# Wider products, a stacked gate operand and one mask for four heads, in a two-layer float32 decoder trunk

## The chip, the cores and the metric

One core of a Trainium2 chip runs the whole program in one launch. The metric is device time in microseconds, the median of several runs. Float32 matrices are multiplied as split pairs: `hi` is the operand rounded to float32r, which TensorE multiplies in a single pass, `lo` is what rounding left, and three products (hi x hi, hi x lo, lo x hi) are added up in PSUM. [...]

## The reference, cut to what matters

The input is 1024 tokens by 1024 features. Layer A is attention with three branches, a pooling mixer and an MLP; layer C is gated linear attention and an MLP. Two places matter here.

```python
# layer A, compressed branch: 63 compressed keys, 8 heads, groups of 4 heads share keys
s_c = einsum('bghqd,bgcd->bghqc', qb, kc)
p_c = masked_softmax(s_c, cmp_end[None, :] <= t[:, None])
o_c = einsum('bghqc,bgcd->bghqd', p_c, vc)

# layer C, projections and decay
h = x @ w_in
q_, k_, v_, r, a = split(h, (512, 512, 1024, 1024, 16))
loga = log_sigmoid(a @ gate_w2 + gate_b) / 16
b = cumsum(loga within a chunk of 64)
q_t, k_t = q * exp(b), k * exp(-b)
...
out = (o * rsqrt(mean(o**2) + eps) * norm_g * silu(r)) @ w_out
```

## The kernel before, in words

The program is written as Python loops on named tiles; a scheduler then sets each engine's order from a model of its own and adds the waits. So a loop's body is not one stretch of the trace: a later step's matmuls may stand between an earlier step's. A tile that has several buffers (`bufs=`) is written again when the last reader of that buffer is done.

**Attention (`attention`, `scores`).** The loops run over 8 query blocks of 128 tokens, two key groups and three branches. In the compressed branch (L483 to L503) the four heads of a group fill a PSUM tile `s` of 4 x 64 columns. `Q2` holds a head's scaled queries split, `hi` on 64 rows and `lo` on the other 64; `K2C` holds the compressed keys twice over the rows, as a rounded part and a rest. So a head takes one product with each part (L489, L490), which multiplies hi and lo of the query at once, and a third (L491), identity times a slice of the constant `cb`, which adds -1e30 to masked keys. `compress` (L387) makes `K2C` with one copy and one subtraction.

**Layer C, its start.** The preceding MLP ends with the first two feature-major weights of layer C. Then `layer_c` opens the pool `wC` and loads what it needs: the decay weights `GW` (16 rows `gate_w2`, one row `gate_b`, L1018 and L1019), the norm gains `ng` (L1021), and then weight after weight. `weight` (L81) loads a piece into a buffer of the tag `rawt`, ACT rounds it into `hit`, DVE subtracts into `lot`. There are 3 buffers of `rawt` and 4 each of `hit` and `lot`. Loads are issued by SP, in order.

**Layer C, projections.** Six feature-major weights (L1059) come first. The token-major ones (L1074) are 8: the first has 272 columns (256 of V and the 16 gate inputs `a`, kept in `A16`), the others 256. Each is cut into two or three pieces of up to 4 x 256 columns. For every weight the loop runs over 8 token blocks; `token_major` issues 24 products (8 blocks of the contraction times three), with the activations stationary and the weight streaming:

```python
for k in range(KB):
    wh, wl = w[k]
    self.mm3(ps, self.xh[half][:, k, ts], self.xl[half][:, k, ts], wh, wl, k == 0, k == KB - 1)
```

Weights 0 to 3 are copied to `VV` by ACT (L1084). Weights 4 to 7 make the output gate: tanh on ACT (L1087), two operations on DVE (L1088, L1089), a store to `gr_d` (L1090).

**Layer C, decay.** With the third weight `decay` (L1023) is called for each token block: TensorE transposes `A16` (L1029), DVE sets `AT` to 1 and copies the transpose into its 16 upper rows, TensorE multiplies `AT` (17 rows) by `GW` in plain float32 (L1034), ACT and DVE take the log-sigmoid, four float32 products with a triangle of ones (L1047) give the cumulative sums, ACT the exponentials, POOL scales queries and keys.

Of the kernel before, what the change touches and what calls it, by code (L numbers as in the profile page):

```python
# [16 lines left out]
P = 128  # L17
S = 1024
D = 1024
# [10 lines left out]
C_ID, C_CAUS, C_WIN, C_CMP, C_T, C_VAL, C_MH, C_INV, C_KEEP, C_N = 0, 128, 256, 384, 512, 643, 644, 645, 709, 837  # L30
# [23 lines left out]
class Body:  # L54
    def __init__(self, tc, io, out):
        self.wbufs = {"rawt": dict(bufs=3), "hit": dict(bufs=4), "lot": dict(bufs=4)}
        self.tc, self.nc, self.io, self.out = tc, tc.nc, io, out
# [153 lines left out]
    def layer_a(self):  # L211
        nc, tc, io, cst, cb = self.nc, self.tc, self.io, self.cst, self.cb
        with ExitStack() as ea:
            self.xa = self.pool(ea, "xa")
            Q2 = [self.xa.tile([P, 8, 512], FR, name=f"Q2_{h}") for h in range(2)]
            K2C = self.xa.tile([P, 2, 2, 64], FR, name="K2C")
            VAC = self.xa.tile([64, 2, P], FR, name="VAC")
            with ExitStack() as ex:
# [4 lines left out]
                psA = self.pool(ex, "psA", bufs=5, space=PSUM)  # L223
# [163 lines left out]
    def compress(self, K2C, VAC, tmp, psA, KC):  # L387
# [10 lines left out]
        nc.vector.memset(K2C[:].bitcast(F32), 0.0)  # L398
        nc.vector.memset(VAC[:].bitcast(F32), 0.0)
        for t in range(2):  # L400
# [26 lines left out]
            if t == 0:  # L427
                nc.tensor.matmul(ps2[:, 0:126], w2[:, 0].rearrange("p a b -> p (a b)"), x[:], start=True, stop=True)
                v = ps2[:, 0:126].rearrange("p (g c) -> p g c", g=2)
                nc.scalar.activation(K2C[:, :, 0, 0:63], v, AF.Copy)  # L430
                nc.vector.tensor_tensor(K2C[:, :, 1, 0:63], v, K2C[:, :, 0, 0:63].bitcast(F32), OP.subtract)
            else:
                for g in range(2):
                    nc.tensor.matmul(ps2[0:63, g * 64:g * 64 + 64], x[:, g * 63:(g + 1) * 63], w2[:, 1, 0], start=True, stop=True)
                v = ps2[0:63, 0:128].rearrange("p (g c) -> p g c", g=2)
                nc.scalar.activation(VAC[0:63, :, 0:64], v, AF.Copy)
                nc.vector.tensor_tensor(VAC[0:63, :, 64:128], v, VAC[0:63, :, 0:64].bitcast(F32), OP.subtract)

    def attention(self, ea, kvp, Q2, K2, VA, gates, CK):
# [4 lines left out]
        with ExitStack() as ex:  # L444
# [28 lines left out]
            def scores(i, g, br):  # L473
# [521 lines left out]
    def layer_c(self, head):  # L995
# [10 lines left out]
        with ExitStack() as ew:  # L1006
# [8 lines left out]
            self.reserve(wp, ("rawt", [P, D], F32, 3), ("hit", [P, D], FR, 4), ("lot", [P, D], FR, 4))  # L1015
# [4 lines left out]
            ng = wp.tile([P, 256], F32, name="ng", bufs=1)  # L1020
            nc.sync.dma_start(ng[:], io["norm_g"].to_broadcast([P, 256]))  # L1021

            def decay(tb):  # L1023
# [50 lines left out]
            for i in range(8):  # L1074
                n, nw = (272, 320) if i == 0 else (256, 256)
                src = io["wC_tm0"] if i == 0 else io["wC_tm"][i - 1]
                w = [(wh[:, 0:n], wl[:, 0:n]) for wh, wl in self.weight(src, [3, 3, 2] if i == 0 else [4, 4], nw, "t")]
                for tb in range(TB):
                    ps = psA.tile([P, 272], F32, name="fm")
# [3 lines left out]
                    if i < 4:  # L1083
                        nc.scalar.activation(VV[tb // 4][:, tb % 4, i * 256:(i + 1) * 256], ps[:, 0:256], AF.Copy)  # L1084
                    else:
                        t = wp.tile([P, 256], F32, name="t", bufs=2)
                        nc.scalar.activation(t[:], ps[:, 0:256], AF.Tanh, scale=0.5)  # L1087
                        nc.vector.scalar_tensor_tensor(t[:], t[:], 1.0, ps[:, 0:256], op0=OP.add, op1=OP.mult)  # L1088
                        nc.vector.scalar_tensor_tensor(t[:], t[:], 0.5, ng[:], op0=OP.mult, op1=OP.mult)  # L1089
                        nc.sync.dma_start(self.gr_d[tb][:, (i - 4) * 256:(i - 3) * 256], t[:])  # L1090
                    if i == 2:
                        decay(tb)
# [150 lines left out]
def lay_out(inputs):  # L1243
# [8 lines left out]
    def km(m):  # L1252
        return m.reshape(KB, P, m.shape[1]).transpose(1, 0, 2)

    io = {}
# [17 lines left out]
    io["wC_tm"] = c(np.stack([km(vr[:, 256 * i:256 * i + 256]) for i in range(1, 8)]))  # L1273
# [33 lines left out]
```

## Time and profile before

| | before |
|---|---|
| three runs | 2336.37, 2332.02, 2336.13 us |
| their median | 2336.13 us |
| profiled execution | 2338.69 us, span 2336.9 us |
| busy: PE, DVE, ACT, POOL | 2248.0, 1469.4, 895.6, 1299.2 us |
| TensorE's mean granted clock | 0.986 of full speed |

Times within the span are counted from its first instruction. A matmul's record is longer than the distance to the next one's start, since matmuls are pipelined. The bracket at a row's end gives the idle time before an instruction and what ended it.

### The profile page before, as it was taken

The page shows a single profiled execution, that of the slowest core. Times are in us where ns is not written, and L with a number is a line of the kernel's source. Part 1 is how long each engine was busy: PE and PEld are TensorE (multiplying, and loading weights), DVE is VectorE, ACT ScalarE, POOL GpSimd, SP SyncE. Part 2 cuts the span into 40 slices and gives each one's busy share as a digit, 9 for nine tenths or more (in the row PEclk, how much of TensorE's full clock was granted, in tenths as well). Part 3 has the DMA queues.
Part 4 walks back from the last instruction along what each step waited for, and adds up shares of the span by engine and source line. Part 5 has one row for each costly group of instructions (what it writes and reads, how often), then busy time and mean ns, then how long its engine had stood idle before and what let it go on. Part 6 is the DMA issues. An engine that isn't in the chain of part 4 may idle for free.

```text
span 2336.9 us, 30957 instructions
## 1 busy us (share of the span) xinstructions
PE 2248.0 (96%) x11346; PEld 1866.6 (80%) x11346; DVE 1469.4 (63%) x2058; ACT 895.6 (38%) x1729; POOL 1299.2 (56%) x955
## 2 busy tenths in 40 slices
PE   8999999998999999999999999989899999999998
PEld 6888777776778877788887999978777888778887
DVE  5622777787766657887671113466676555788776
ACT  4213766664333333444322255222242333344431
POOL 2112766563867765989750012043385776588884
PEclk9999999999999999999999999999999999999999
DMA  5144110004454455644232211222445445474421
GB/s 185 46 145 139 48 41 13 10 10 165 163 162 150 152 200 184 222 142 146 65 129 63 78 37 57 65 105 73 176 153 167 149 149 201 158 258 140 145 73 72
DMA packets 121417, 282.42 MB, mean 121 GB/s; under 512 B 13985, under 2 KB 19361, under 8 KB 121266
## 3 DMA queue, kind: packets, MB, share of 16 engines
q1 hardware_dynamic: 113202, 259.48, 33.6%
q10 hardware_dynamic: 8064, 20.98, 2.4%
q8 instruction: 89, 1.46, 0.3%
q14 instruction: 62, 0.51, 0.1%
HBM read 197.57 MB, written 80.74 MB: 119 GB/s over the span
## 4 chain that ended last, share of the span: by engine, by line
PE 42%; POOL 4%; issue 3%; DVE 2%; DMA 2%; ACT 1%; ACTq 0%; POOLq 0%; SPq 0%; DVEq 0%
PE u L105 6%; PE u L103 6%; PE u L104 6%; PE fm L105 4%; PE fm L103 4%; PE fm L104 4%; PE v L105 3%; PE v L103 3%; PE v L104 3%; POOL op L76 2%; POOL T L902 1%; DVE op L76 1%; PE y L103 1%; PE y L104 1%; PE y L105 1%
## 5 line engine op out<-in xcount | busy, mean ns | idle before, releaser
L76 POOL TENSOR_TENSOR op<-a,op 128x512 fp32r<-128x512 f32 x168 | 272.0, 1642 | 61.3 <-ACT op L75 54.4
L75 ACT ACTIVATE op<-a 128x512 fp32r<-128x512 f32 x168 | 104.3, 621 | 189.6 <-issue 135.5
L105 PE MATMUL u<-op 128*128 128x512 f32 x448 | 173.1, 392 | 3.3 <-POOL op L76 3.2
L104 PE MATMUL u<-op 128*128 128x512 f32 x448 | 171.9, 390 | 1.4 <-DVE op L76 1.4
L103 PE MATMUL u<-op 128*128 128x512 f32 x448 | 170.1, 390 | 0.7 <-DVE XT L918 0.7
L105 PE MATMUL u<-Bt,op 128*128 128x512 f32 x384 | 151.0, 394 | 5.1 <-DVE op L76 5.1
L75 ACT ACTIVATE op<-S 128x512 fp32r<-128x512 f32 x144 | 90.5, 629 | 169.6 <-PE u L105 97.5
L103 PE MATMUL u<-Bt,op 128*128 128x512 f32 x384 | 151.3, 394 | 4.0 <-ACT ev L713 4.0
L104 PE MATMUL u<-Bt,op 128*128 128x512 f32 x384 | 150.7, 392 | 0.0
L105 PE MATMUL fm<-hit,xl 128*128 128x256 f32 (+1 forms) x512 | 145.9, 285 | 0.0
L103 PE MATMUL fm<-hit,xh 128*128 128x256 f32 (+1 forms) x512 | 145.8, 285 | 0.0
L104 PE MATMUL fm<-lot,xh 128*128 128x256 f32 (+1 forms) x512 | 145.0, 283 | 0.0
L76 DVE TENSOR_TENSOR op<-T,op 128x512 fp32r<-128x512 f32 x96 | 117.8, 1233 | 23.8 <-ACT op L75 23.8
L104 PE MATMUL v<-op 128*128 128x512 f32 x336 | 130.1, 390 | 2.4 <-DVE op L76 2.4
L105 PE MATMUL v<-op 128*128 128x512 f32 x336 | 129.9, 390 | 0.6 <-POOL op L76 0.6
L1053 POOL TENSOR_TENSOR QK<-QK,E 128x512 f32<-128x512 f32 x8 | 10.4, 1305 | 209.8 <-ACT E L1049 200.9
L103 PE MATMUL v<-op 128*128 128x512 f32 x336 | 125.7, 390 | 1.0 <-ACT op L75 1.0
L76 POOL TENSOR_TENSOR low<-raww,hiw 128x1024 fp32r<-128x1024 f32 (+1 forms) x22 | 40.6, 1860 | 143.5 <-ACT hiw L75 143.5
L705 POOL TENSOR_TENSOR S<-raw 128x512 f32<-128x512 f32 x64 | 95.7, 1502 | 44.4 <-DVE op L76 42.7
L918 DVE TENSOR_TENSOR XT<-XT,u 128x512 f32<-128x512 f32 x144 | 95.3, 678 | 29.8 <-PE u L105 29.4
L75 ACT ACTIVATE op<-raw 128x512 fp32r<-128x512 f32 x116 | 71.4, 627 | 108.9 <-PE v L105 80.8
L727 DVE SCALAR_TENSOR_TENSOR ev<-ev 128x512 f32<-128x512 f32 x96 | 111.1, 1158 | 2.1
(377 smaller groups left out, 6997.2 us busy)
## 6 DMA issues: line engine op xcount, KB each, us to landing
raw<-in_w_dram SPq DMA_DIRECT2D x72, 512.0 KB, 3.8
S_d<-ev SPq DMA_DIRECT2D x112, 256.0 KB, 2.3
w2r<-in_w_dram SPq DMA_DIRECT2D x56, 512.0 KB, 4.5
A_d<-ev SPq DMA_DIRECT2D x100, 256.0 KB, 2.5
a<-S_d SPq DMA_DIRECT2D x96, 256.0 KB, 2.7
a<-A_d SPq DMA_DIRECT2D x88, 256.0 KB, 2.8
x_d<-xt ACTq DMA_DIRECT2D x16, 512.0 KB, 2.6
raw<-x_d SPq DMA_DIRECT2D x16, 512.0 KB, 4.5
```

The source lines that it names most:

```text
L75: nc.scalar.activation(hi, src, AF.Copy)
L76: (lo_eng or nc.vector).tensor_tensor(lo, src, hi.bitcast(F32), OP.subtract)
L103: mm(out, lh, rh, start=start, stop=False, **kw)
L104: mm(out, lh, rl, start=False, stop=False, **kw)
L105: mm(out, ll, rh, start=False, stop=stop, **kw)
L705: POOL.tensor_tensor(st[p][name], st[p][x], st[p][y], op)
L727: DVE.scalar_tensor_tensor(other[:], other[:], 0.0, other[:], op0=OP.max, op1=OP.mult)
L902: sb[0].tensor_tensor(*sb[1:])
L918: DVE.tensor_tensor(x, x, ps[:], add)
L1053: nc.gpsimd.tensor_tensor(q1, q1, E1[:], OP.mult)
```

## The change

1. **Compressed scores.** `K2C` becomes one float32 tile. For a group one mask product of 256 columns opens the accumulation (the mask's slice is repeated for four heads by its access pattern), and a head takes one product in plain float32 (the query tile is read as float32). `compress` loses the subtraction.
2. **Gate product.** `GW` becomes 96 rows of float32r: rounded weights at row 0 and at row 32, the rest at row 64; unused rows are zero. They are built once, by way of a buffer of the tag `rawt` that is set to zero, filled by six loads, rounded by ACT and subtracted by DVE. `AT` becomes two standing tiles of 96 rows: rounded inputs at 0 and 64, the rest at 32, with ones beside the rounded parts for the bias. One float32r product of 96 rows takes the place of the float32 one of 17.
3. **Token-major weights.** Weights 2 to 7 (256 columns) become three of 512, loaded in four pieces of 2 x 512 columns. What follows them (copy, tanh, the two operations with `ng`, the store) is 512 columns wide; `ng` is loaded twice, side by side. `rawt` has 2 buffers now, `hit` and `lot` 5.

```diff
-        self.wbufs = {"rawt": dict(bufs=3), "hit": dict(bufs=4), "lot": dict(bufs=4)}
+        self.wbufs = {"rawt": dict(bufs=2), "hit": dict(bufs=5), "lot": dict(bufs=5)}
...
+                    mask = cb[:, None, C_CMP + 64 - 8 * i:C_CMP + 128 - 8 * i].to_broadcast([P, 4, 64])
+                    nc.tensor.matmul(s[:, 0:256].rearrange("p (h c) -> p h c", h=4), idb, mask, start=True, stop=False)
                     for hp in range(4):
-                        o = s[:, hp * 64:(hp + 1) * 64]
                         q = Q2[half][:, g * 4 + hp, qs]
-                        nc.tensor.matmul(o, q, K2C[:, g, 0], start=True, stop=False)
-                        nc.tensor.matmul(o, q, K2C[:, g, 1], start=False, stop=False)
-                        nc.tensor.matmul(o, idb, cb[:, C_CMP + 64 - 8 * i:C_CMP + 128 - 8 * i], start=False, stop=True)
+                        nc.tensor.matmul(s[:, hp * 64:(hp + 1) * 64], q.bitcast(F32), K2C[:, g], start=False, stop=hp == 3)
...
-            GW = wp.tile([17, 512], F32, name="GW", bufs=1)
-            nc.sync.dma_start(GW[0:16], io["gate_w2"])
-            nc.sync.dma_start(GW[16:17], io["gate_b"])
...
+            GW = wp.tile([96, 512], FR, name="GW", bufs=1)
+            gw = wp.tile([P, D], F32, name="gw", tag="rawt", bufs=2)
+            nc.vector.memset(gw[0:96, 0:512], 0.0)
+            for r in (0, 32, 64):
+                nc.sync.dma_start(gw[r:r + 16, 0:512], io["gate_w2"])
+                nc.sync.dma_start(gw[r + 16:r + 17, 0:512], io["gate_b"])
+            nc.scalar.activation(GW[:], gw[0:96, 0:512], AF.Copy)
+            nc.vector.tensor_tensor(GW[64:96], gw[64:96, 0:512], GW[64:96].bitcast(F32), OP.subtract)
...
-                AT = wp.tile([17, P], F32, name="AT", bufs=1)
-                nc.vector.memset(AT[:], 1.0)
-                nc.vector.tensor_copy(AT[0:16], ps[0:16, 0:P])
+                AT = ATs[tb % 2]
+                nc.scalar.activation(AT[0:16], ps[0:16, 0:P], AF.Copy)
+                nc.scalar.activation(AT[64:80], ps[0:16, 0:P], AF.Copy)
+                nc.vector.tensor_tensor(AT[32:48], ps[0:16, 0:P], AT[0:16].bitcast(F32), OP.subtract)
...
-            for i in range(8):
...
+            for i, (c, n, nw, ks) in enumerate(((0, 272, 320, [3, 3, 2]), (256, 256, 256, [4, 4])) + tuple((512 * j, 512, 512, [2] * 4) for j in (1, 2, 3))):
+                src = io["wC_tm0"] if i == 0 else io["wC_tm1"] if i == 1 else io["wC_tm"][i - 2]
+                w = [(wh[:, 0:n], wl[:, 0:n]) for wh, wl in self.weight(src, ks, nw, "t")]
```

The scheduler's order at three places, of the program before and of the changed one.

On SP, where layer C starts (`rawt` the raw weights, `wo` the output weights of later), before:

```order
L1070 DMA wo<-in_w_out_c_dram 128x2x1024 x3
L1018 DMA GW<-in_gate_w_dram 16x512
L1019 DMA GW<-in_gate_b_dram 1x512
L1021 DMA ng<-in_norm_g_dram 128x256
L87 DMA rawt<-in_wC_fm_dram 128x512 x12
L87 DMA rawt<-in_wC_tm_dram 128x960 x2
```

and changed:

```order
L1081 DMA wo<-in_w_out_c_dram 128x2x1024 x3
L1031 DMA ng<-in_norm_g_dram 128x256 x2
L1020 DMA gw<-in_gate_w_dram 16x512
L1021 DMA gw<-in_gate_b_dram 1x512
L1020 DMA gw<-in_gate_w_dram 16x512
L1021 DMA gw<-in_gate_b_dram 1x512
L1020 DMA gw<-in_gate_w_dram 16x512
L1021 DMA gw<-in_gate_b_dram 1x512
L87 DMA rawt<-in_wC_fm_dram 128x512 x12
L87 DMA rawt<-in_wC_tm_dram 128x960 x2
```

Six small loads by way of `gw` now stand between the early loads and the first weight; `ng` moved ahead of them.

On PE, where a later weight's first token block ends, with buffer numbers (`fm` the PSUM tile of a token block, `hit` and `lot` the weight's split pieces), before:

```order
L105 MATMUL fm_12590<-hit_12585,xl0_10694 128x256
L103 MATMUL fm_12590<-hit_12585,xh0_10693 128x256
L104 MATMUL fm_12590<-lot_12586,xh0_10693 128x256
L105 MATMUL fm_12590<-hit_12585,xl0_10694 128x256
L103 MATMUL fm_12616<-hit_12579,xh0_10693 128x256
L104 MATMUL fm_12616<-lot_12580,xh0_10693 128x256
L105 MATMUL fm_12616<-hit_12579,xl0_10694 128x256
```

and changed, in the second weight of 512 columns, whose pieces are `hit_12495`, `12501`, `12507` and `12513`:

```order
L104 MATMUL fm_12548<-lot_12496,xh0_10580 128x512
L105 MATMUL fm_12548<-hit_12495,xl0_10581 128x512
L103 MATMUL fm_12548<-hit_12495,xh0_10580 128x512
L104 MATMUL fm_12548<-lot_12496,xh0_10580 128x512
L105 MATMUL fm_12548<-hit_12495,xl0_10581 128x512
L103 MATMUL fm_12548<-hit_12501,xh0_10580 128x512
L104 MATMUL fm_12548<-lot_12502,xh0_10580 128x512
L1045 MATMUL d_12255<-GW_11172,AT1_11184 128x512
L105 MATMUL fm_12548<-hit_12501,xl0_10581 128x512
L103 MATMUL fm_12548<-hit_12501,xh0_10580 128x512
L103 MATMUL fm_12518<-hit_12513,xh0_10580 128x512
```

Before, a block's 24 products follow each other. Now 18 products of the first block have gone, then 10 of the next block and a gate product, before the first one with the fourth piece, `hit_12513`.

On PE, in the compressed scores of a group (`s` the PSUM tile, `cb` the masks), before:

```order
L489 MATMUL s<-K2C,Q_0_244 128x64
L490 MATMUL s<-K2C,Q_0_244 128x64
L491 LDWEIGHTS cb
L491 MATMUL s<-cb 128x64
L489 MATMUL s<-K2C,Q_0_244 128x64
L490 MATMUL s<-K2C,Q_0_244 128x64
L491 LDWEIGHTS cb
L491 MATMUL s<-cb 128x64
```

and changed:

```order
L524 MATMUL s<-cb 128x128
L486 LDWEIGHTS cb
L486 MATMUL s<-cb 128x256
L489 MATMUL s<-K2C,Q_0_244 128x64 x4
L521 MATMUL s<-K2s,Q_0_244 128x256
L522 MATMUL s<-K2s,Q_0_244 128x256
```

Three instructions for each head became one, and four masks one of 256 columns ahead of them.

## Rows read from the trace of the kernel before

**Rows 1.** The page, part 1: busy us, share of the span, instructions.

```profile
PE 2248.0 (96%) x11346; PEld 1866.6 (80%) x11346; DVE 1469.4 (63%) x2058; ACT 895.6 (38%) x1729; POOL 1299.2 (56%) x955
```

**Rows 2.** Windows by time: length, busy us of each engine, PE clock, DMA, GB/s.

```profile
225.00:540.00 315.00, 299.01 (x1820) 235.84 (x1818) 242.34 (x471) 204.54 (x465) 199.07 (x219) 0.98 0.09 33
...
1308.10:1511.40 203.30, 203.30 (x1626) 195.96 (x1624) 55.84 (x107) 82.64 (x166) 20.90 (x16) 1.00 0.16 52
```

**Rows 3.** Timeline of PE: start, us, engine, line, operation; 38 rows between.

```profile
1299.24 0.39 PE L105 MATMUL fm<-xh,lot 128*128 128x512 f32 x1
...
1308.08 0.39 PE L105 MATMUL fm<-xh,lot 128*128 128x512 f32 x1
```

**Rows 4.** Timeline of ACT: one L1087 for each block of 24 narrow products.

```profile
1456.96 0.38 ACT L1087 ACTIVATE t<-fm 128x256 f32<-128x256 f32 x1 [2.13 <-PE fm L105]
...
1464.16 1.06 ACT L75 ACTIVATE hit<-rawt 128x1024 fp32r<-128x1024 f32 x1 [1.06 <-PE fm L105]
...
1511.68 0.38 ACT L1087 ACTIVATE t<-fm 128x256 f32<-128x256 f32 x1 [2.49 <-PE fm L105]
```

**Rows 5.** Timeline of PE around one gate product, L1034.

```profile
1361.01 0.28 PE L104 MATMUL fm<-lot,xh 128*128 128x256 f32 x1
1361.22 1.12 PE L1034 MATMUL d<-GW,AT 17*128 17x512 f32 x2
1362.27 0.39 PE L105 MATMUL fm<-hit,xl 128*128 128x256 f32 x1
1362.49 0.28 PE L103 MATMUL fm<-hit,xh 128*128 128x256 f32 x1
```

**Rows 6.** Timeline of PE, two products of 64 rows.

```profile
521.25 0.51 PE L554 MATMUL o<-th,VAC 64*128 64x512 f32 x1
521.60 0.40 PE L555 MATMUL o<-tl,VAC 64*128 64x512 f32 x1
```

**Rows 7.** Timeline of PE, one head's compressed scores and the next's first.

```profile
231.45 0.28 PE L489 MATMUL s<-K2C,Q 128*128 128x64 f32 x1
...
231.68 0.21 PE L491 MATMUL s<-cb 128*128 128x64 bf16 x1
231.72 0.28 PE L489 MATMUL s<-K2C,Q 128*128 128x64 f32 x1
```

**Rows 8.** Timeline of PE, four float32 products (eight records), the next start.

```profile
1443.64 1.06 PE L1047 MATMUL d<-cst,t__12557 128*128 128x131 f32 x8
1444.45 0.36 PE L103 MATMUL fm<-hit,xh 128*128 128x256 f32 x1
```

**Rows 9.** Timeline of the SP queue before layer C: issues of loads.

```profile
1212.98 0.69 SPq L1018 DMA_DIRECT2D GW<-in_gate_w_dram  x1
1213.72 0.30 SPq L1019 DMA_DIRECT2D GW<-in_gate_b_dram  x1
...
1236.40 8.93 SPq L87 DMA_DIRECT2D rawt<-in_wC_fm_dram  x7
```

**Rows 10.** Timeline of PE, first products of layer C; 13 rows between.

```profile
1240.17 0.80 PE L103 MATMUL fm<-xh,hit 128*128 128x512 f32 x1 [3.71 <-ACT hit L75]
...
1246.15 0.39 PE L103 MATMUL fm<-xh,hit 128*128 128x512 f32 x1
```

**Rows 11.** Chain of waits after the last token-major block: start, us, what.

```profile
1511.68 0.39 ACT t L1087
1512.09 0.43 DVE t L1088
...
1513.17 0.50 DVE att L1110
```

**Rows 12.** Groups on DVE, 1308 to 1512 us: busy us, mean ns | idle.

```profile
L76 DVE TENSOR_TENSOR lot<-rawt,hit 128x1024 fp32r<-128x1024 f32 x14 | 17.9, 1286 | 32.1 <-ACT hit L75 32.1
...
L1039 DVE SCALAR_TENSOR_TENSOR t__12179<-d,t__12179 128x512 f32<-128x512 f32 x1 | 0.7, 692 | 3.2 <-ACT t__12179 L1038 3.2
```

**Rows 13.** DMA issues, 1308 to 1512 us: xcount, KB, us to landing.

```profile
rawt<-in_wC_tm_dram SPq DMA_DIRECT2D x11, 512.0 KB, 4.3
```

More of the change, by code (lines that the diff above doesn't have):

```diff
@@ L215, in layer_a @@
             Q2 = [self.xa.tile([P, 8, 512], FR, name=f"Q2_{h}") for h in range(2)]
-            K2C = self.xa.tile([P, 2, 2, 64], FR, name="K2C")
+            K2C = self.xa.tile([P, 2, 64], F32, name="K2C")
             VAC = self.xa.tile([64, 2, P], FR, name="VAC")
@@ L397, in compress @@
             nc.sync.dma_start(w2[:, :, d], io["cmp_w2"])
-        nc.vector.memset(K2C[:].bitcast(F32), 0.0)
+        nc.vector.memset(K2C[:], 0.0)
         nc.vector.memset(VAC[:].bitcast(F32), 0.0)
@@ L1014, in layer_c @@
             psD = self.pool(ew, "psD", bufs=3, space=PSUM)
-            self.reserve(wp, ("rawt", [P, D], F32, 3), ("hit", [P, D], FR, 4), ("lot", [P, D], FR, 4))
+            self.reserve(wp, ("rawt", [P, D], F32, 2), ("hit", [P, D], FR, 5), ("lot", [P, D], FR, 5))
             A16 = wp.tile([P, TB, 16], F32, name="A16", bufs=1)
-            GW = wp.tile([17, 512], F32, name="GW", bufs=1)
-            nc.sync.dma_start(GW[0:16], io["gate_w2"])
-            nc.sync.dma_start(GW[16:17], io["gate_b"])
-            ng = wp.tile([P, 256], F32, name="ng", bufs=1)
-            nc.sync.dma_start(ng[:], io["norm_g"].to_broadcast([P, 256]))
+            GW = wp.tile([96, 512], FR, name="GW", bufs=1)
[6 more added lines that the diff above has]
+            nc.vector.tensor_tensor(GW[64:96], gw[64:96, 0:512], GW[64:96].bitcast(F32), OP.subtract)
+            ATs = [wp.tile([96, P], FR, name=f"AT{j}", bufs=1) for j in range(2)]
+            for t in ATs:
+                for r, one in ((0, 1.0), (32, 0.0), (64, 1.0)):
+                    nc.vector.memset(t[r:r + 32].bitcast(F32), one)
+            ng = wp.tile([P, 512], F32, name="ng", bufs=1)
+            for j in range(2):
+                nc.sync.dma_start(ng[:, j * 256:(j + 1) * 256], io["norm_g"].to_broadcast([P, 256]))
             def decay(tb):
@@ L1073, in layer_c @@
                 preload_wo()
-            for i in range(8):
-                n, nw = (272, 320) if i == 0 else (256, 256)
-                src = io["wC_tm0"] if i == 0 else io["wC_tm"][i - 1]
-                w = [(wh[:, 0:n], wl[:, 0:n]) for wh, wl in self.weight(src, [3, 3, 2] if i == 0 else [4, 4], nw, "t")]
+            for i, (c, n, nw, ks) in enumerate(((0, 272, 320, [3, 3, 2]), (256, 256, 256, [4, 4])) + tuple((512 * j, 512, 512, [2] * 4) for j in (1, 2, 3))):
+                src = io["wC_tm0"] if i == 0 else io["wC_tm1"] if i == 1 else io["wC_tm"][i - 2]
+                w = [(wh[:, 0:n], wl[:, 0:n]) for wh, wl in self.weight(src, ks, nw, "t")]
                 for tb in range(TB):
-                    ps = psA.tile([P, 272], F32, name="fm")
+                    ps = psA.tile([P, 512], F32, name="fm")
                     self.token_major(w, ps[:, 0:n], tb)
@@ L1082, in layer_c @@
                         nc.vector.tensor_copy(A16[:, tb], ps[:, 256:272])
[L1083 to L1088 removed]
+                        n_ = 256
+                    else:
+                        n_ = n
+                    if i < 3:
+                        nc.scalar.activation(VV[tb // 4][:, tb % 4, c:c + n_], ps[:, 0:n_], AF.Copy)
+                    else:
+                        t = wp.tile([P, 512], F32, name="t", bufs=2)
+                        nc.scalar.activation(t[:], ps[:], AF.Tanh, scale=0.5)
+                        nc.vector.scalar_tensor_tensor(t[:], t[:], 1.0, ps[:], op0=OP.add, op1=OP.mult)
                         nc.vector.scalar_tensor_tensor(t[:], t[:], 0.5, ng[:], op0=OP.mult, op1=OP.mult)
[L1090 removed]
+                        nc.sync.dma_start(self.gr_d[tb][:, c - D:c - D + 512], t[:])
                     if i == 2:
@@ L1272, in lay_out @@
     io["wC_tm0"] = c(km(np.concatenate([vr[:, 0:256], al, np.zeros((D, 48), np.float32)], axis=1)))
-    io["wC_tm"] = c(np.stack([km(vr[:, 256 * i:256 * i + 256]) for i in range(1, 8)]))
+    io["wC_tm1"] = c(km(vr[:, 256:512]))
+    io["wC_tm"] = c(np.stack([km(vr[:, 512 * i:512 * i + 512]) for i in range(1, 4)]))
     io["gate_w2"] = c(a["c_gate_w2"][0])
```

3 lines of the change are left out of this document (1 added, 2 removed).

## The prediction

> **What bounds the kernel now.** I read the page's busy times first: TensorE is busy for 96% of the span [rows 1], so a change pays where it shortens the matmul stream, or costs where that stream must wait. Next I cut the span into stages by time [rows 2]: attention, which holds the compressed scores, has TensorE busy for 299 of 315 us; the token-major projections of layer C have it busy for all of 203.3 us, at a granted clock of 1.00, which is the upper of its two levels, 2.4 GHz. In the second stage nothing else is late, so there each nanosecond off a matmul is a nanosecond off the run. Last came the matmul timeline, read by the distance between starts: durations overlap (0.28 us is shown for products that start every 0.12 us), so a sum of durations would overstate everything. The sum is made against the profiled execution, 2338.69 us (span 2336.9 us and 1.8 us around it). It stands 2.6 us above the median of the three runs, 2336.13 us. A measurement of this kernel tells 0.2%, about 4.7 us, from no change.
>
> **The 512-column weights.** Six weights of 256 columns become three of 512: 6 x 8 token blocks x 24 = 1152 products become 576. One block of 24 narrow products lasts 2.88 us (nineteen of them between the two outer rows, 1456.96 and 1511.68 us) [rows 4], so 0.120 us each. At 512 columns with the same split tiles the distance is (1308.08 - 1299.24) / 39 = 0.2267 us [rows 3]. These are feature-major products: the weight is stationary there and the activation streams, in token-major it is the other way round, but both are 128 rows by 128 columns of the same type. Two narrow ones cost 0.2400 us, one wide one 0.2267: 0.0133 us saved, times 576 is **-7.7 us**. Both widths thus carry about 13.3 ns besides their columns at 2.4 GHz (256 columns are 106.7 ns, 512 are 213.3).
>
> The Trainium skill (TensorE: Matmul & The Clock Gate, section "Back-to-back issue gap") gives that fixed part as about 2.5 ns; by it halving the count would save 576 x 2.5 ns = 1.4 us. The trace disagrees with it at both widths, and I go by the trace.
>
> The copies and gate products on ACT, DVE and the queue become half as many and twice as wide. They lie beside the matmuls (ACT is busy for 83 of the 203 us, DVE for 56 [rows 2]), so I cost them at nothing, except the last one, below.
>
> **The gate product.** A plain float32 product of 17 rows and 512 columns stands in the matmul stream eight times. From the product before it (1361.01) to the second after it (1362.49) pass 1.48 us [rows 5]; without it two steps of 0.12 us would: it costs 1.24 us. Now it is one single-pass product of 96 rows. No row shows 96 rows. Bounds: a full-height product, 0.227 us [rows 3]; and above, a product of 64 rows, which takes 0.35 us until the next start [rows 6], plus 0.09 us on each side for changing height (0.21 instead of 0.12 us before it, 0.22 after it [rows 5]): 0.53 us. I take 0.43 us, one such change, because the 64-row product is the nearest row and its 0.35 us already hold one. Saved 0.81 us, times 8: **-6.5 us** (bounds -5.7 and -8.1). The two copies and the subtraction that build the stacked operand stand on ACT and DVE between the transpose and this product; the changed order leaves products of other tiles between them, and a decay now recurs every 60 to 70 wide products, some 15 us, where it recurred after some 70 narrow ones. I cost them at nothing; if that cover failed, each would add about 0.5 us on TensorE.
>
> The Trainium skill (the same page, section "LDWEIGHTS (loading the stationary operand)") has the weight load depend on columns alone, not on rows. By it 96 rows cost what 128 do, 0.227 us, and the term would be -8.1 us; the 64-row product's 0.35 us speaks against that here.
>
> **The compressed scores.** Before, a head took two products of 64 columns and a mask: 231.45 to 231.72, 0.27 us, so 1.08 us for four heads [rows 7]. Each product takes 0.115 us, far above 64 columns' time, so its weight load must set it. A plain float32 product has two records. Four of them with 131 columns last 0.81 us until the next start [rows 8], 0.10 us per record; with 64 columns no more, and no less than the two single loads they replace unless those get cheaper. So four heads cost 0.81 to 0.92 us, the change of type behind them 0.09 (as on each side of the gate product [rows 5]), and one mask of 256 columns 0.107 to 0.16: 1.01 to 1.17 against 1.08 us. **0 us**, bounds -1.1 and +1.4 over 16 groups. The scheduler also moves neighbours around these products. With 16 us of gaps in this stage that could go either way; I leave 3 us to each side.
>
> **The start of layer C.** The gate weights used to have a small tile of their own, loaded at 1213 us. Now they pass through a buffer of the weight tag `rawt`, and in the built program the memset of that buffer waits for a matmul that stands twelve products before the end of the preceding MLP. Behind it on SP stand six small loads, and behind these the first weight load of layer C, which in the old order was issued at 1236.40 us [rows 9], with TensorE idle until its weight came. Twelve products at 0.12 us are 1.44 us and the old load also waited for the same stream's end, so the memset starts near 1235.1; a DVE memset of 512 columns takes 0.50 us [rows 11]; SP starts near 1235.7. A pair of small loads took 0.69 + 0.30 us with the gap between them, 1.05 us [rows 9]; the long one may have been slowed by 3 MB in flight, so the pair lies between 0.7 and 1.1 us. Three pairs, 2.1 to 3.3 us; the first weight is issued at 1237.8 to 1239.0, I take 1238.6: **+2.2 us** (bounds +1.4 and +2.6). It lands after the rounding of the gate weights on ACT, so that adds nothing. The clock already falls in today's wait of 3.71 us and comes back at 1246.15 [rows 10]; I expect the same after the longer one.
>
> **The end of the projections.** The chain of waits goes on from the last block through ACT and DVE: tanh, two products, memset [rows 11]. They become twice as wide: ACT 0.39 to 0.60 us (+0.2), DVE 0.43 to 0.69 us twice (+0.5; 0.69 is a 128x512 operation of the same kind [rows 12]). What is late next is the same DVE queue. **+0.7 us**, bounds +0.4 and +1.0.
>
> **Sum:** -7.7 - 6.5 + 0 + 2.2 + 0.7 = -11.3 us: 2327.4 against the profiled execution, 2324.8 against the median. I predict **2325 us**.
>
> **The rivals.**
> *The refill holds up the stream (slower).* Each wide weight has four tiles, and there are five buffers for the split tiles and two for raw ones, so the fourth tile is loaded only after the second has been split, and that only after the last token block has freed a buffer. From the start of that block: 6 products (1.36 us), ACT 1.06 [rows 4], DVE 1.29 [rows 12], the load 4.3 [rows 13], ACT 1.06, DVE 1.29: 10.4 us. It is needed after 24 + 18 products of the two blocks and 11 that the new order pulls in between, 12.0 us, plus about 1.0 for a decay: 13.0. The margin is 2.6 us; it is used up when ACT, a strict queue, has a decay with both of its table loads ahead of the split. For: those stand there in the changed order, right ahead of the fourth tile's split. Against: ACT is busy for 41% of the stage, and those exponentials are due before the tile has landed. Each of three refills would then lose some 2.5 us, and the clock's return after a wait about 2.8 us more (14 products at 0.43 instead of 0.23 us [rows 10]): 16 us, 2341 us. Chance 0.06.
> *The width saves only a fixed 2.5 ns per product* [against: rows 3, 4]: 6.3 us less gain, 2331 us. Chance 0.05. It is the case of the skill's rule above.
> *The gate product stays dear:* 96 rows taken in two passes, or its operand late. Half of the gain goes: 2328 to 2331 us. Chance 0.08.
> *Attention is reshuffled for the worse or the better* by more than 3 us, since the moved masks shift what runs beside them: 2330 or 2320 us. Chance 0.05 each.
> *It does not do what it says:* the built program has the fewer, wider products, so I give this no chance of its own.
>
> **How the numbers follow.** My forecast has 0.71. Its own bounds: the gains reach from -15.8 to -13.4 us, attention from -4 to +4, start and handover from +1.8 to +3.6, which makes 2318 to 2331 with all ends added up. The range takes in the width and gate rivals: 2317 to 2333 us. Left out are the refill and the outer ends. Faster by over 0.2% means under 2331.5: the forecast, the better attention, and most of the gate and width cases, 0.82; within 0.2%: 0.11; slower: 0.07.
>
> **What would show it.** In the new profile: wide products at 0.227 us in the token-major stage and a stage near 189 us; the gate product's neighbours 0.4 to 0.5 us further apart than a step; the first weight of layer C issued about 2 us later against the end of the MLP; the attention stage within 3 us of 315. The prediction is wrong if TensorE waits for ACT's split tiles inside the token-major stage, if wide products come every 0.24 us, or if attention moves by more than 4 us.

## The result, and the profile after

The changed kernel takes 2322.24 us (median of five runs, 2321.39 to 2323.91) against 2336.13 us: a ratio of 0.9939, 95% interval 0.9923 to 0.9956, which is 10 to 18 us. The forecast was 2325 us, 2317 to 2333. The profiled execution took 2323.91 us with a span of 2322.1 us, 14.8 us under that of before.

Part 1 of its page shows 632 products fewer (576 of the weights, 48 of the scores, 8 of the gate) and TensorE still busy for 96% [rows 1]:

```profile
PE 2230.2 (96%) x10714; PEld 1831.6 (79%) x10714; DVE 1465.5 (63%) x2025; ACT 896.8 (39%) x1722; POOL 1296.4 (56%) x955
```

The windows by time answer to [rows 2]: attention over the same stretch, and the token-major stage, which now ends after 188 us and is still busy throughout at the upper clock.

```profile
225.00:540.00 315.00, 297.64 (x1787) 233.77 (x1786) 242.46 (x473) 205.15 (x467) 198.97 (x219) 0.99 0.10 36
...
1307.20:1495.20 188.00, 188.00 (x1041) 164.57 (x1040) 47.22 (x67) 82.32 (x157) 20.45 (x16) 1.00 0.16 55
```

To see where the time went I cut both profiled executions at the starts of the same products (timeline of TensorE; attention is cut at its third product from the last):

| stage | before, us | after, us | difference | forecast |
|---|---|---|---|---|
| layer A's projections | 226.84 | 227.61 | +0.8 | 0 |
| attention | 315.98 | 312.55 | -3.4 | 0 (-4 to +4) |
| MLP | 693.35 | 694.60 | +1.3 | 0 |
| last MLP product to first of layer C | 4.00 | 5.15 | +1.2 | +2.2 |
| feature-major products | 68.13 | 67.32 | -0.8 | 0 |
| token-major products | 203.06 | 187.76 | -15.3 | -14.2 |
| last token-major product to the first of the output projection | 26.18 | 27.26 | +1.1 | +0.7 |
| the rest, to TensorE's last product | 790.45 | 790.37 | -0.1 | 0 |

The token-major stage gave more than forecast, attention gave something, and two stages whose products the change does not touch (layer A, the MLP) took back 2 us. The times of the table fall by 15.4 us; 0.6 us came back behind TensorE's last product, which leaves the 14.8 us of the span.

The gate product, L1045, in the timeline of TensorE, answers to [rows 5]: it starts 0.22 us after the product before it, and the next starts 0.24 us later. It takes one ordinary step.

```profile
1363.57 0.39 PE L104 MATMUL fm<-lot,xh 128*128 128x512 f32 x1
1363.80 0.39 PE L105 MATMUL fm<-hit,xl 128*128 128x512 f32 x1
1364.02 0.40 PE L1045 MATMUL d<-GW,AT 96*128 96x512 f32 x1
1364.26 0.40 PE L103 MATMUL fm<-hit,xh 128*128 128x512 f32 x1
```

One group of compressed scores, L486 and L489, answers to [rows 7]: from the mask to the next other product 0.93 us instead of 1.08. The mask takes 0.11, the eight records 0.82 (two for each plain float32 product).

```profile
238.32 0.27 PE L486 MATMUL s<-cb 128*128 128x256 bf16 x1
238.43 1.00 PE L489 MATMUL s<-K2C,Q 128*128 128x64 f32 x8
239.25 0.36 PE L521 MATMUL s<-K2s,Q 128*128 128x256 f32 x1
239.45 0.28 PE L522 MATMUL s<-K2s,Q 128*128 128x256 f32 x1
```

The first product behind the group takes 0.20 us until the next start. Behind a group of the kernel before it does too:

```profile
239.95 0.36 PE L523 MATMUL s<-K2s,Q 128*128 128x256 f32 x1
240.15 0.28 PE L524 MATMUL s<-K2s,Q 128*128 128x256 f32 x1
```

The start of layer C, timelines of DVE, SP and TensorE, answers to [rows 9, 10]: memset, six small loads, and then, at 1236.40, the first weight; TensorE, done with the MLP's last product at 1235.0, waits 4.87 us.

```profile
1233.78 0.48 DVE L1018 MEMSET gw<- 96x512 f32 x1 [3.97 <-PE v L105]
...
1234.29 0.34 SPq L1020 DMA_DIRECT2D gw<-in_gate_w_dram  x1
...
1236.40 8.55 SPq L87 DMA_DIRECT2D rawt<-in_wC_fm_dram  x5
...
1239.91 0.80 PE L103 MATMUL fm<-xh,hit 128*128 128x512 f32 x1 [4.87 <-ACT hit L75]
```

The handover from the projections to the recurrence, timelines of DVE, POOL and TensorE, answers to [rows 11]. The second product with Dc on DVE (L1148, which writes a buffer of `q2`) waits 0.80 us for a DMA, the write of the last gate rows `t`. Meanwhile POOL begins to split the output weights (L76), and the product on DVE then takes 2.25 us instead of 0.6 to 0.7: it ends 0.55 us after POOL's operation. Behind it on DVE stand the copies into `att` (L1153), and for these TensorE waits 4.01 us. It starts the first product with `att` 7.99 us after the last token-major product (1494.99).

```profile
1496.77 0.69 DVE L1103 SCALAR_TENSOR_TENSOR t<-t,ng 128x512 f32<-128x512 f32 x1
...
1498.59 0.63 DVE L1148 TENSOR_TENSOR q<-QK,Dc 128x512 f32<-128x512 f32 x1
1499.37 2.35 POOL L76 TENSOR_TENSOR WL<-wo,WH 128x1024 fp32r<-128x1024 f32 x1 [21.13 <-ACT WH L75]
1500.02 2.25 DVE L1148 TENSOR_TENSOR q<-QK,Dc 128x512 f32<-128x512 f32 x1 [0.80 <-DMA gr_d<-t]
1502.20 1.36 DVE L1153 COPY_PREDICATED att<-keep,a 128x512 f32<-128x512 uint32 x2
...
1502.98 3.38 PE L1178 MATMUL o<-V,att 128*128 128x256 f32 x8 [4.01 <-DVE att L1153]
```

Before, both products with Dc (L1134) ran without a wait, and the first one with `att` came 4.91 us after the last token-major product:

```profile
1511.36 0.28 PE L105 MATMUL fm<-hit,xl 128*128 128x256 f32 x1
1514.11 1.22 DVE L1134 TENSOR_TENSOR q<-QK,Dc 128x512 f32<-128x512 f32 x2
1516.27 1.03 PE L1164 MATMUL o<-V,att 128*128 128x256 f32 x4
```

### The profile page after: what moved, and what is told of

Same layout as the page of the kernel before. It is cut to its first block, busy times and chain, and to the rows that moved or that the text cites. A ratio compares the mean times of both kernels' runs of the same rounds, so it can differ in the third digit from the quotient of the medians.

```text
span 2322.1 us, 29592 instructions
## 1 busy us (share of the span) xinstructions
PE 2230.2 (96%) x10714; PEld 1831.6 (79%) x10714; DVE 1465.5 (63%) x2025; ACT 896.8 (39%) x1722; POOL 1296.4 (56%) x955
## 5 line engine op out<-in xcount | busy, mean ns | idle before, releaser
L76 POOL TENSOR_TENSOR op<-a,op 128x512 fp32r<-128x512 f32 x168 | 272.3, 1645 | 60.5 <-ACT op L75 51.3
L76 DVE TENSOR_TENSOR op<-T,op 128x512 fp32r<-128x512 f32 x96 | 120.5, 1262 | 24.0 <-ACT op L75 24.0
L76 POOL TENSOR_TENSOR low<-raww,hiw 128x1024 fp32r<-128x1024 f32 (+1 forms) x22 | 40.9, 1870 | 144.0 <-ACT hiw L75 144.0
L75 ACT ACTIVATE th<-pt 128x512 fp32r<-128x512 f32 (+1 forms) x148 | 86.1, 599 | 66.3 <-PE pt L548 39.0
L105 PE MATMUL fm<-hit,xl 128*128 128x512 f32 (+2 forms) x320 | 111.4, 349 | 0.0
L104 PE MATMUL fm<-lot,xh 128*128 128x512 f32 (+2 forms) x320 | 111.3, 348 | 0.0
```

The source lines that it names most:

```text
L75: nc.scalar.activation(hi, src, AF.Copy)
L76: (lo_eng or nc.vector).tensor_tensor(lo, src, hi.bitcast(F32), OP.subtract)
L104: mm(out, lh, rl, start=False, stop=False, **kw)
L105: mm(out, ll, rh, start=False, stop=stop, **kw)
```

## The experiments

My theory: three independent savings in the matmul stream, a loss at the start of layer C and one at the handover. The rivals differ for each part and stand in the expectations. Ratios are against the kernel before, run on the same chip.

### One part of the change at a time

The 512-column weights alone: the kernel before with

```
-        self.wbufs = {"rawt": dict(bufs=3), "hit": dict(bufs=4), "lot": dict(bufs=4)}
+        self.wbufs = {"rawt": dict(bufs=2), "hit": dict(bufs=5), "lot": dict(bufs=5)}
...
-            for i in range(8):
+            for i, (c, n, nw, ks) in enumerate(((0, 272, 320, [3, 3, 2]), (256, 256, 256, [4, 4])) + tuple((512 * j, 512, 512, [2] * 4) for j in (1, 2, 3))):
```

> The kernel before with the 512-column token-major weights alone (and the buffer counts that belong to them). If a product carries some 13 ns besides its columns, 576 products fewer save 7.7 us: the token-major stage of layer C falls from 203.1 to about 195.4 us (last product against first), and with about 1 us given back at the handover to the recurrence the kernel gains 6.7 us, 2329.4 us. If the fixed part is 2.5 ns, as the Trainium skill's page has it, the stage falls by 1.4 us only and the kernel does not move (2334 to 2337 us).

Measured: 2327.2 us, ratio 0.9951 (0.9939 to 0.9964), 9.3 us under the 2336.53 of before. The token-major stage took 195.92 us, 7.1 less: the width term stands (7.7 forecast, 1.4 by its rival), with 12.4 ns for each product left out. The rest was not expected: the wait ahead of layer C fell to 2.41 us and the feature-major stage to 66.91. The first weight load is issued 1.25 us ahead of the MLP's last product (1235.60), in the kernel before 0.23 us after it (1236.17) [rows 9], though this kernel has nothing new there (timelines of SP and TensorE):

```profile
1234.35 10.40 SPq L87 DMA_DIRECT2D rawt<-in_wC_fm_dram  x6
...
1238.01 0.79 PE L103 MATMUL fm<-xh,hit 128*128 128x512 f32 x1 [2.13 <-ACT hit L75]
```

In the built program that load waits for the product 13 before the MLP's last; before, for the one right before the last. The pool has grown by 7 KB, so its first raw buffer lies lower, over another of the MLP's last weights, one that is done with earlier.

The gate product alone: the kernel before with

```
-            GW = wp.tile([17, 512], F32, name="GW", bufs=1)
...
+            GW = wp.tile([96, 512], FR, name="GW", bufs=1)
+            gw = wp.tile([P, D], F32, name="gw", tag="rawt", bufs=3)
```

> The kernel before with the stacked gate product alone, its operand passing through the buffer of the raw weights. If 96 rows cost what 128 rows do, the product takes one step of 0.23 us instead of 1.24 us: the token-major stage falls by 8.1 us to 195.0, and less 0.4 to 1.2 us at the start of layer C the kernel gains about 7 us, 2329 us. If the forecast's 0.43 us per product were right, the stage would fall by 6.5 us and the kernel by 4.3 to 5.3, about 2331 us.

Measured: 2324.66 us, ratio 0.9939 (0.9926 to 0.9953), 11.9 us under before (the profiled execution was the longest of five, 2331.68). The token-major stage took 195.01 us, 8.05 less or 1.01 per product: 96 rows cost a full step. Here too the start of layer C is shorter, wait 1.49 and feature-major 66.01 us, in spite of the detour of the gate weights (memset and six loads by way of `gw`): `gw` takes the first raw buffer, and the first weight gets the second, which lies over nothing that the MLP's end still needs. Its load is issued 22 us ahead of the MLP's last product, past the detour.

```profile
1219.06 0.70 SPq L87 DMA_DIRECT2D rawt<-in_wC_fm_dram  x1
...
1242.92 0.50 PE L103 MATMUL fm<-xh,hit 128*128 128x512 f32 x1 [1.20 <-ACT hit L75]
```

The compressed scores alone: the kernel before with

```
+                    nc.tensor.matmul(s[:, 0:256].rearrange("p (h c) -> p h c", h=4), idb, mask, start=True, stop=False)
...
+                        nc.tensor.matmul(s[:, hp * 64:(hp + 1) * 64], q.bitcast(F32), K2C[:, g], start=False, stop=hp == 3)
```

> The kernel before with the compressed scores alone. If their gain is in the products (a group of four heads 0.93 us instead of 1.08), sixteen groups give 2.4 us, attention is shorter by 2.4 to 3.5 us, the groups read 0.93 us again, and the kernel gains 2 to 4 us, about 2333 us. If the 3.5 us by which attention was shorter in the changed kernel came from products that the scheduler happened to move, attention here differs from that by more than 1.5 us one way or the other.

Measured: 2335.91 us, ratio 0.9993 (0.9984 to 1.0002), 0.6 us under before and at most 3.7. Most groups read 0.92 to 0.96 us again, attention 312.52. At 0.15 us a group the products are cheaper by 16 x 0.15 = 2.4 us, and by some 2 us over all groups, which were not alike before (0.99 to 1.11 us at the upper clock); that the kernel gains it was not shown.

By the medians the three gains add up to 21.8 us and the whole change gave 13.9 (by the ratios some 27 and 14). From the MLP's last product to the end of the feature-major stage the kernels took 72.1 us (before), 69.3 (width), 67.5 (gate), 72.0 (scores), 72.5 (all). The first two gained 2.8 and 4.6 us there that the whole does not have, having lost 0.3 us itself: 7.8 us of the 8 to 13 that are missing. That stretch is read from one execution each, and what the rest is was not shown. In the whole change the pool lies as in the first and the detour stands ahead of the first weight, as it doesn't in the second.

### The height of the gate product

The changed kernel with

```
-            GW = wp.tile([96, 512], FR, name="GW", bufs=1)
+            GW = wp.tile([64, 512], FR, name="GW", bufs=1)
...
-                nc.scalar.activation(AT[64:80], ps[0:16, 0:P], AF.Copy)
```

> The changed kernel with the gate product 64 rows high instead of 96: the stacked part with the low half of the gate weights is left out, so that much precision of the gate. If the height of 64 rows is what costs (as two products of 64 rows showed it in attention), each gate product takes about 0.43 us until the next start instead of 0.23, and the token-major stage is longer by 8 x 0.2 = 1.6 us, 189.4 instead of 187.8. If rows cost nothing at any height, the step stays 0.23 us and the stage 187.8, and what attention showed is something else, such as the change between types.

Measured: 2324.79 us (two runs); the stage took 190.74 us, 2.98 more or 0.37 per product. Timeline of TensorE:

```profile
1361.24 0.39 PE L104 MATMUL fm<-lot,xh 128*128 128x512 f32 x1
1361.56 0.50 PE L1043 MATMUL d<-GW,AT 64*128 64x512 f32 x1
1361.98 0.50 PE L105 MATMUL fm<-hit,xl 128*128 128x512 f32 x1
1362.32 0.39 PE L103 MATMUL fm<-hit,xh 128*128 128x512 f32 x1
```

The product ahead takes 0.32 us until the next start, the 64 rows 0.42, the product behind 0.34, each 0.23 otherwise. The 0.42 was expected, what the neighbours pay was not. In attention two products of 64 rows can stand side by side, in the changed kernel for example:

```profile
257.39 0.40 PE L565 MATMUL o<-tl,VA 128*128 128x512 f32 x1
257.71 0.50 PE L552 MATMUL o<-th,VAC 64*128 64x512 f32 x1
258.05 0.39 PE L553 MATMUL o<-tl,VAC 64*128 64x512 f32 x1
258.38 0.44 PE L560 MATMUL pt<-cst,pw 128*128 128x128 f32 x2
```

The three steps, 0.32 to 0.34 us each, are 0.30 us over three of 0.23, for two products of 64 rows; the lone one above costs 0.37 on average. So the price goes with the change to another height and back, not with the number of 64-row products, and 96 rows do not pay it. The Trainium skill (TensorEngine Tiling (Array Packing), section "Key Properties") says that a change of tiling mode drains the engine; in its section "Available Configurations" the modes have tiles of 128, 64 and 32 rows. These rows agree: 96 behave as 128, 64 as a mode of their own, for 0.30 to 0.37 us there and back.

### The form of the scores

The kernel before with one float32 product per head, the four masks kept:

```
-                        nc.tensor.matmul(o, q, K2C[:, g, 0], start=True, stop=False)
-                        nc.tensor.matmul(o, q, K2C[:, g, 1], start=False, stop=False)
+                        nc.tensor.matmul(o, q.bitcast(F32), K2C[:, g], start=True, stop=False)
```

> The kernel before with the one float32 product per head, but the four masks of 64 columns kept between the heads. If a change of type between neighbours costs some 0.09 us each time, four heads take 4 x (0.20 + 0.04 + 0.09) = 1.3 us, more than the 1.08 before, and the kernel is slower by 2 to 5 us: then the gain of the scores needs the one mask. If only the number of weight loads counts, four heads take 4 x 0.24 = 0.96 us and attention is shorter by about 2 us, as in the whole change.

Measured: 2330.36 us, ratio 0.9977 (0.9968 to 0.9987). A miss on both sides: four heads take mostly 1.03 to 1.09 us, as before, and yet it was 5.4 us faster by the ratio. Its execution showed a granted clock of 1.00 between 227 and 250 us, where the kernel before had 0.78, and attention took 310.18 us. So I put the same form into the changed kernel:

```
-                    nc.tensor.matmul(s[:, 0:256].rearrange("p (h c) -> p h c", h=4), idb, mask, start=True, stop=False)
...
+                        nc.tensor.matmul(s[:, hp * 64:(hp + 1) * 64], idb, cb[:, C_CMP + 64 - 8 * i:C_CMP + 128 - 8 * i], start=False, stop=True)
```

> The changed kernel with the four masks of 64 columns back between the float32 score products. The groups take about 1.06 us instead of 0.93, 2 us in all. If the gain of that form on the kernel before came from a start of attention without a fall of the clock, the granted clock between 227 and 250 us is 1.00 here too instead of 0.86, attention is 1 to 3 us shorter in spite of the dearer groups, and the kernel at 2318 to 2321 us. If it was the spread between executions, the kernel is slower than the changed one by about 2 us, 2324 us.

Measured: 2322.51 us, ratio 0.9938 (0.9924 to 0.9952), as the changed kernel; the clock in that stretch was 0.78. In this execution the form did not keep the clock up there. The traces show another stretch, though: in the MLP, after a wait of 2.0 us that all kernels have, the granted clock was 1.00 in both executions with this form (859 to 866 and 861 to 868 us), where the kernel before had 0.76 (865 to 872) and the changed one 0.76 (863 to 870), and the MLP took 690.99 and 689.88 us instead of 692.7 to 695.7 in the others. Two executions do not tell whether the form or chance did that, so why it gained on the kernel before stays open.

### The losses of the change

The write of `t` at the handover: the changed kernel with the buffers of the recurrence in another order.

```
-            self.reserve(gp, ("lng", [P, D], F32, 1), ("lnb", [P, D], F32, 1),
+            self.reserve(gp, ("q2", [P, 4, P], F32, 2), ("kt", [P, 512], F32, 2),
...
+            self.reserve(gp, ("lng", [P, D], F32, 1), ("lnb", [P, D], F32, 1))
```

> The changed kernel with the two q2 and the two kt buffers of the recurrence laid where no buffer of the last gate rows (t) lies; the LN constants lie there instead. In the changed kernel the second q2 waits for the write of the last t to memory, and the copies into att stand behind it on DVE. If that wait is the loss of the handover, the first product with att starts about 5.5 us after the last wide product instead of 8.0 us, and the kernel gains 1.0 to 2.3 us (2320 to 2321 us). If the DVE work itself is the bound, the start moves by under 0.7 us and the kernel not at all.

`q2` holds the queries scaled by the decay, `kt` the transposed keys.

Measured: 2320.54 us, ratio 0.9927 (0.9915 to 0.994). The first product with `att` starts 5.53 us after the last wide one (1496.06), and the output projection 23.79 us after it instead of 27.26. No wait for a DMA is left on DVE, and both products with Dc are short again:

```profile
1499.66 1.22 DVE L1149 TENSOR_TENSOR q<-QK,Dc 128x512 f32<-128x512 f32 x2
1500.80 1.36 DVE L1154 COPY_PREDICATED att<-keep,a 128x512 f32<-128x512 uint32 x2
...
1501.59 1.99 PE L1179 MATMUL o<-V,att 128*128 128x256 f32 x8 [1.61 <-DVE att L1154]
```

The median gained 1.7 us on the changed kernel, too little to tell by runs alone; the 2.5 us at the first product with `att` are the trace's.

The detour of the gate weights:

```
-            gw = wp.tile([P, D], F32, name="gw", tag="rawt", bufs=2)
+            gw = wp.tile([P, 512], F32, name="gw", tag="E1", bufs=1)
```

> The changed kernel with the gate weights passing through the buffer of E1 instead of a raw weight's. If the wait of that buffer for the preceding MLP is what delays the first weight load of layer C, the memset and the six loads stand some 20 us earlier, TensorE waits about 3.7 us again instead of 4.9, and the kernel gains 0.3 to 1.2 us. If the first weight load waits for the end of the MLP by itself as late as that, the wait stays 4.9 us and nothing moves.

Measured: 2316.3 us, ratio 0.9909 (0.9896 to 0.9923). From the MLP's last product to layer C's first 2.13 us instead of 5.15: the first weight is issued 1.25 us before that last product starts (1232.63), in the changed kernel 1.64 us after it.

```profile
1231.38 12.51 SPq L87 DMA_DIRECT2D rawt<-in_wC_fm_dram  x7
...
1234.76 0.50 PE L103 MATMUL fm<-xh,hit 128*128 128x512 f32 x1 [1.85 <-ACT hit L75]
```

So the detour costs 3.0 us, and the lower place of the raw buffers hides 1.9 of it (4.00 to 2.13). The expectation missed: the six loads stand only 6 us earlier (1228.24), the wait fell further than to 3.7 us, and the kernel gained 5.9 us instead of at most 1.2. Not all of that is the detour. The output projection also starts 24.64 us after the last wide product instead of 27.26, at a place where this edit has no aim: the second product with Dc waits for its DMA here too, but it begins ahead of POOL's operation and takes 0.69 us.

```profile
1494.55 0.69 DVE L1148 TENSOR_TENSOR q<-QK,Dc 128x512 f32<-128x512 f32 x1 [0.75 <-DMA gr_d<-t]
1494.70 2.78 POOL L76 TENSOR_TENSOR WL<-wo,WH 128x1024 fp32r<-128x1024 f32 x1 [21.87 <-ACT WH L75]
```

In the changed kernel and four others POOL's operation begins first, and whenever the product with Dc starts there (4.88 to 5.03 us after the last wide product), it ends at 7.28 or 7.29. So the loss of the handover has two parts, the wait of 0.8 us and some 1.6 us behind POOL that the wait lets in.

### What the height of 96 rows gives elsewhere

The changed kernel with attention's 32 products of 64 rows (L552, L553) padded with zeros:

```
-                        nc.tensor.transpose(pt[0:64, hp * P:(hp + 1) * P], Ps[:, hp], ident)
-                    self.split(th[0:64], tl[0:64], pt[0:64])
+                        nc.tensor.transpose(pt[0:96, hp * P:(hp + 1) * P], Ps[:, hp], ident)
+                    self.split(th[0:96], tl[0:96], pt[0:96])
```

> The changed kernel with the 32 compressed value products of attention padded from 64 to 96 rows with zeros (the probabilities transposed as 96 columns, 32 of them zero). If 64 rows cost because of their height and 96 run like 128, each takes 0.1 to 0.2 us less until the next start, 3 to 5 us in all: attention is shorter by 3 to 5 us and the kernel at 2317 to 2319 us. If the height costs nothing, attention stays within 1 us and the 16 small memsets on POOL are all that is new: 2322 to 2323 us.

Measured: 2318.84 us, ratio 0.9919 (0.9905 to 0.9932), attention 308.36 us. One of the products in the changed kernel, timeline of TensorE:

```profile
314.98 0.23 PE L524 MATMUL s<-cb 128*128 128x128 bf16 x1
315.14 0.50 PE L553 MATMUL o<-tl,VAC 64*128 64x512 f32 x1
315.57 1.09 PE L560 MATMUL pt<-cst,p 128*128 128x128 f32 x8
```

and here:

```profile
313.03 0.23 PE L526 MATMUL s<-cb 128*128 128x128 bf16 x1
313.07 0.48 PE L555 MATMUL o<-tl,VAC 96*128 96x512 f32 x1
313.40 1.04 PE L562 MATMUL pt<-cst,p 128*128 128x128 f32 x8
```

0.04 instead of 0.16 us ahead of it, 0.33 instead of 0.43 behind. More rows are cheaper. The medians, 3.4 us apart, do not settle the gain alone; attention does: 305.3 to 308.4 us in the three kernels with padded products (two of them below), 312.5 to 315.0 in the five with the same products at 64 rows.

### All three together

The changed kernel with the last three edits:

> The changed kernel with three edits at once: the gate weights through E1's buffer, the recurrence's q2 and kt buffers away from t, and the value products of the compressed branch 96 rows high. If each takes out a loss of its own (3.0 us of waiting ahead of layer C, 2.5 to 3.5 us at the handover, some 4 us in attention), the kernel is at 2312 to 2315 us: the wait ahead of layer C about 2.1 us, the first product with att 5.5 us after the last wide one. If they share one cover, as when the scheduler or a fall of the clock takes back what one gives, it stays above 2316 us.

Measured: 2308.41 us, ratio 0.9878 (0.9864 to 0.9892): 14 us under the changed kernel, as much again as the change itself gave, and below the 2312 expected. Wait 2.13 us, first product with `att` 5.54 us after the last wide one, attention 305.34. That is 3.0 us less than with the padding alone; nothing shows a reason, and executions of one stream of products differ by as much (last section).

The same aims by another layout of the pool:

```
+            self.reserve(wp, ("E1", [P, 512], F32, 1), ("E2", [P, 4, P], F32, 1), ("t_", [P, 512], F32, 1), ("ng", [P, 512], F32, 1), ("t", [P, 512], F32, 2),
+                         ("A16", [P, TB, 16], F32, 1), ("AT0", [96, P], FR, 1), ("AT1", [96, P], FR, 1), ("GW", [96, 512], FR, 1),
+                         ("rawt", [P, D], F32, 2), ("hit", [P, D], FR, 5), ("lot", [P, D], FR, 5))
```

> The same three aims, but reached by laying out the buffers of layer C's projections otherwise: what is needed late (E1, E2, t_, ng, t, A16, AT, GW) lies where the MLP's last weights lay, the raw and split weight buffers above them, and the gate weights are loaded behind the first four weight loads, with their memsets on POOL. If the place of the first raw buffer sets the start of layer C, its first load is issued some 20 us before the MLP ends, the wait is 1.2 to 1.6 us (the last copy of the MLP's products on ACT stands ahead), the feature-major stage about 66 us because the clock hardly falls, and the kernel is 1.5 to 2.5 us below the one with the three edits. If the load's time in memory or the DVE work sets it, the wait stays above 2 us.

Measured: 2308.69 us, ratio 0.988 (0.9864 to 0.9896). The place does set the start: the first load is issued 23 us ahead of the MLP's last product (1231.19), wait 1.48 and feature-major 65.41 us, 2.3 less together than with the three edits.

```profile
1207.95 1.32 SPq L87 DMA_DIRECT2D rawt<-in_wC_fm_dram  x2
...
1232.67 0.50 PE L103 MATMUL fm<-xh,hit 128*128 128x512 f32 x1 [1.20 <-ACT hit L75]
```

The median did not follow. In this execution the handover took 1.8 us longer, with the same starts up to 19.8 us and then products at the lower clock's pace for longer; attention took 2.9 us longer. What the layout gives lies below what runs of these two kernels tell apart.

## Why the prediction was right, and where its steps were not

The time fell 2.8 us below the forecast and inside its range. Step by step:

- **The 512-column weights**, -7.7 us: right, 7.1 us with that part alone. The fixed 13.3 ns per product, worked out from [rows 3, 4], nearly held: 12.4 ns for each product left out. The Trainium skill (TensorE: Matmul & The Clock Gate, section "Back-to-back issue gap") gives 2.5 ns for an isolated product, an estimate of 1.4 us here; the stage does not agree.
- **The gate product**, -6.5 us: the size was off; measured -8.05, the far bound. The step that failed is "the 64-row product is the nearest row" [rows 6]. It is nearest in number, but what it pays is the change of height, and 96 rows change nothing: 0.24 us until the next start instead of the 0.43 I took. The Trainium skill's rule that the weight load depends on columns alone (TensorE: Matmul & The Clock Gate, section "LDWEIGHTS (loading the stationary operand)") gave the right number at 96 rows. Of the 0.37 us that a product of 64 rows cost more, neighbours included, it says nothing.
- **The compressed scores**, 0 us: the sign was open, and the products came out at 0.93 us a group, below my lower end of 1.01. The step that failed is the 0.09 us for the change of type behind them: the product behind the old group pays it too (239.95 to 240.15 before, 239.25 to 239.45 after), so it is no difference. Of the 2.4 us that this makes over sixteen groups, the kernel with the scores alone shows 0.6, at most 3.7. The 3.4 us by which attention was shorter in the profiled execution do not stand out from what executions differ by.
- **The start of layer C**, +2.2 us: measured +1.2. Against the MLP's last product the first weight was issued 1.4 us later than before, my lower end, since the six loads took 2.1 us. The detour itself was undersized (3.0 us), and a gain that I had not looked for, the lower place of the first raw buffer, gave back 1.9. With the feature-major stage the net was +0.3. I read which product the memset waits for, but not why: the address.
- **The end of the projections**, +0.7 us: +1.1 in this execution, in agreement by luck. My chain, wider operations on ACT and DVE, cost what I said: the first product with Dc starts 3.60 us after the last token-major product instead of 2.75. Behind it comes what I had not seen, the wait for the write of `t` and the product held up beside POOL, 2.5 us that a new place for two buffers removed. The first product with `att` is thus 3.1 us late, and how much of that reaches the output projection differs: with the wait and the operation of over 2.2 us it started 25.4 to 27.4 us after the last wide product in five kernels, against 25.6 to 26.2 in the four that have neither and narrow weights.
- **The rivals**: nowhere in the token-major stage does TensorE wait; it is busy for 188.00 of 188.00 us, so the refill never held it up.

Too large a loss at the start and too small a gain at the gate product and in attention thus make up more than the 2.8 us by which the forecast was high; the 2 us lost in untouched stages lie the other way. That the total came this near is in part luck.

## What to carry to other kernels

Price a matmul by the steps of its neighbours as well as its own: a product of 64 rows among products of 128 cost on both sides here, one of 96 rows did not, and padding 64 rows to 96 can pay. When a buffer count changes, look at which old buffers the new addresses lie over, since the first load or the first write waits for the last reader there. A short wait can cost more than its length, when another engine's operation gets in ahead. Parts of a change that each win alone need not add up where they share one wait.

## What the runs showed of the chip

The same instructions in the same order are granted different clocks in different executions. The changed kernel and three of its variants have the same products in the same order up to layer C. Between 227 and 250 us (windows by time) the granted clock was, in the changed kernel,

```profile
227.00:250.00 23.00, 19.19 (x120) 15.27 (x119) 12.49 (x41) 15.47 (x56) 17.48 (x30) 0.87 0.28 92
```

with the gate weights through E1's buffer

```profile
227.00:250.00 23.00, 19.18 (x132) 14.82 (x130) 14.63 (x47) 17.33 (x62) 18.70 (x33) 1.00 0.28 93
```

with the recurrence's buffers moved

```profile
227.00:250.00 23.00, 20.27 (x119) 17.01 (x118) 13.13 (x42) 16.33 (x59) 17.49 (x30) 0.78 0.28 93
```

Attention took 312.55, 312.88 and 314.97 us in these three. The kernel before and its two variants with the old scores, alike up to layer C too, span 313.44 to 320.51 us. So one execution tells a stage that waits often from another only to some 3 us, and in the kernel before to 7; the token-major stage, which never waits, was 187.76 us in all seven kernels that share it.
